# A fused attention and recurrent layer: where the sums of projection weight blocks are made

## The chip, the cores and the metric

The kernel runs on one core of a Trainium2 chip. The metric is the device time of one execution in microseconds (us). The engines are TensorE (PE for its matmuls, PEld for its weight loads), VectorE (DVE), ScalarE (ACT), GpSimd (POOL) and SyncE (SP); SP issues most DMAs, POOL the rest.

## The reference

One decoder layer on a sequence of 512 tokens with a width of 1024, in float32:

```python
h = rmsnorm(x, norm_mix_g)
q, k, v, xr, gr, g_attn, g_rnn = split(h @ w_in)              # 7 x 1024 columns
attn_out = diff_attention(q, k, v, ...)                       # 8 heads
rnn_out  = rg_lru_branch(xr, gr, conv_w, ..., w_a, w_x, ...)  # conv, two block-diagonal gates, scan, gelu
y_attn = attn_out @ w_proj_attn                               # 1024 x 1024
y_rnn  = rnn_out @ w_proj_rnn
merged = sigmoid(g_attn) * y_attn + sigmoid(g_rnn) * y_rnn
x = x + merged @ w_out
x = x + relu(rmsnorm(x) @ w_up)**2 @ w_down                   # 1024 x 4096 and back
```

## The kernel before, in words

Every matrix operand is split into a high and a low part (`hi` is a cast to a shorter format, `lo = x - hi`), and a product is three matmuls: hi by hi, hi by lo, lo by hi (`mm3`). Weights arrive in units of 128 x 1024 floats, 512 KB. A unit goes through three steps: SP loads it into one of two buffers `wraw`, ACT casts it to `whi`, DVE subtracts to get `wlo`. There are four buffers for pairs of `whi` and `wlo`, and a pair is free again when the unit's matmuls are done.

The kernel has these stages in order: a head (loads, norm), the attention with the projections of q, k, v and the two merge gates (45 to 283 us of the profiled execution), the stretch behind the attention, here called the recurrent stage (function `recurrent`, 291.45 us to about 476 us), the product with `w_out` and the norm (to about 520 us), and the MLP (to the end).

The recurrent stage lays several streams of PE work beside each other: 16 column units of `w_in` for xr and gr (`x` and `g` in the string `seq`), the attention's projection (`y`), the matmuls of the recurrence's gates (`t`), the projection of the recurrent branch (`a`, `b`, `c`) and the first units of `w_out` (`o`). PE's order is written out by hand in `seq`. The order of DVE, ACT and SP comes from a planner (`Plan`): each task has an engine, a duration, the tasks it follows, and places that it takes (2 of "raw" for the `wraw` buffers, 4 of "unit" for the pairs, 8 of "bank" for the accumulators `acc`). It computes when each task is due for PE, lays the tasks out by that, tries random changes, and emits the instructions in the order of the best layout. All engines then run their instructions in that fixed order and wait on semaphores. `HOPS` and `MARGIN` are the planner's cost of going from engine to engine and its reserve ahead of PE; `dve` and `act` are its durations.

The attention's projection (`project`) multiplies by blocks: the weight of one half of the output columns is four blocks b0, b1, b2, b3 (`w_pa[n, 0..3]`, each one unit), and instead of eight block products it takes seven, M1 to M7. M1, M2 and M3 use the plain blocks b0, b2 and b3. The other four use sums of blocks: M5 is b0+b1, M6 is b0+b1+b3, M4 is b0+b1+b3+b2, M7 is b1+b3. The matching sums of the activations (`early`, `third`, `pair_forms`) are made on DVE.

In the kernel before, POOL makes the sums of the weights while the attention runs. `add_up` loads a block from `w_pa` into an SBUF tile `sum`, adds the next block by an accumulating DMA into the same tile, and stores the tile to DRAM tensors `pa0M5`, `pa0M6` and so on (lists `pa_sums`). One generator per half takes turns (`in_turn`, `pas`), one step at a time, at fixed points of `qkv_pair` and `attention`. That makes 12 loads and 8 stores of 512 KB. In the recurrent stage each half then loads seven units: three plain ones and four finished sums.

A similar chain on POOL, `weight_sums`, makes 12 sums for the MLP's first weight with 18 loads and 12 stores into `up2M`, `up4M`, `up6M`. It starts behind the first convolution step of chunk 0 (`first` in `chunk`, line 1215). Its SBUF tile `sum` lies in a pool that is closed behind the recurrent stage.

The recurrence's gate weights come in four pairs of loads of 128 KB, one pair per chunk of the recurrent width (`graw`, line 1194). They land in a buffer of their own, `graw`, and are cast to `gw0` on ACT and subtracted to `gw1` on DVE.

Of the kernel before, what the change touches and what calls it, by code (L numbers as in the profile page):

```python
# [13 lines left out]
F32 = mybir.dt.float32  # L14
# [7 lines left out]
P = 128  # L22
# [17 lines left out]
def tile_block(ctx: ExitStack, tc: tile.TileContext, x, w_in, w_rga, w_rgx, w_pa, w_pr, w_o,  # L40
# [7 lines left out]
    sm = ctx.enter_context(tc.tile_pool(name="sm", bufs=4))  # L48
# [167 lines left out]
    def in_turn(*gs):  # L216
        gs = list(gs)
        while gs:
            g = gs.pop(0)
            if next(g, gs) is not gs:  # L220
                gs.append(g)
                yield

# [56 lines left out]
    ORDER_Y = ("M1", "M2", "M5", "M6", "M7", "M3", "M4")  # L280
    PLAIN = {"M1": 0, "M2": 2, "M3": 3}
# [9 lines left out]
    pa_sums = [{p: dp.tile([P, 1024], F32, name=f"pa{n}{p}") for p in ("M5", "M7", "M6", "M4")} for n in range(2)]  # L291
# [13 lines left out]

    def add_up(w, into):
        t = unit("sum", F32).rearrange("p c s -> p (c s)")
        for blocks in CHAINS:
            for b, p in blocks:
                if p:  # L310
                    G.dma_start(t, w[b], accum_op=ALU.add)
                    yield
                    G.dma_start(into[p], t)
                else:
                    G.dma_start(t, w[b])
                yield
# [224 lines left out]
    def qkv_pair(j, qk, v):  # L541
# [50 lines left out]
        for o, qi, gsc in ((OK_, 1, kg), (OQ, 0, qg), (OV, None, None)):  # L592
            t = -1
            for more in proj(o, banks[o]):
# [25 lines left out]
                if j == 0 and t % 2 == 1:  # L620
                    next(pas)
# [3 lines left out]
    def attention(fills, qks, vs, pads):  # L625
# [176 lines left out]
        for step in range(max(acts) + 1):  # L802
# [10 lines left out]
            for n, f in enumerate(order):  # L813
# [140 lines left out]
    HOPS = lambda x, t: 0.06 + (MARGIN if t.engine == "PE" else 0.0) if x.engine != t.engine else x.us - x.land  # L954
    MARGIN = 0.7
    dve = lambda columns: 0.08 + 0.00107 * columns
    act = lambda columns: 0.1 + 0.00085 * columns

    def recurrent(rp):
# [10 lines left out]
        class Unit:  # L970


            def __init__(self, src, shift, have=None, raw=None):
                self.raw, self.pair = raw, have
# [6 lines left out]
                if have or raw:  # L981
                    load.begun = -20.0
# [7 lines left out]
            def high(self):  # L990
                self.pair = weight_pair(self.shift)
                A.copy(self.pair[0], self.raw)
# [1082 lines left out]
```

## Time and profile before

| what | value |
|---|---|
| times of three runs | 836.78, 839.27 and 2138.16 us, median 839.27 |
| time of the profiled execution | 834.94 us, its span 833.2 us |
| granted TensorE clock | 1.00 |
| PE busy, share of the span | 824.5 us, 99% |
| DVE busy | 678.0 us, 81% |
| ACT busy | 502.4 us, 60% |
| POOL busy | 113.2 us, 14% |
| recurrent stage, 291.45 to 475.70 us | PE 181.81 of 184.25 us, DVE 155.05, ACT 119.26 |
| POOL's loads from `w_pa` in the attention | 12, first issued at 53.3 us, last at 143.2 us |
| POOL's loads from `w_up` in the recurrent stage | 18, first issued at 303.2 us, last at 464.8 us |

The table is read by stage. A busy time of PE below the stage's length is time in which PE waited for something; the trace's view of waits names what ended each such wait. Busy times of DVE and ACT say how much those engines have to do beside PE in the same stretch, not whether they are on the path.

### The profile page before, as it was taken

Reading aid. Unit: us, or ns where it says so; the run is one execution under the profiler, and the core shown is the slowest. Engines: PE = TensorE matmul, PEld = TensorE weight load, DVE = VectorE, ACT = ScalarE, POOL = GpSimd, SP = SyncE. Lnnn points to the kernel's source line nnn. Section 1 sums busy time; section 2 is a strip of 40 time slices with the busy share of each in tenths; the row PEclk is TensorE's granted clock in tenths of the full one; section 3 lists DMA queues with packets and bytes.
Section 4 is the critical chain, followed back from the end, with each engine's and each line's share of the span. In section 5 each row is a group of like instructions: output and inputs, shape, how many; then the busy total and the mean of one; then the engine's idle time right before and its main releaser. Section 6 shows DMA issues by size and latency. Waiting matters only on the chain.

```text
span 833.2 us, 14735 instructions
## 1 busy us (share of the span) xinstructions
PE 824.5 (99%) x5788; PEld 763.1 (92%) x5788; DVE 678.0 (81%) x1092; ACT 502.4 (60%) x791; POOL 113.2 (14%) x146
## 2 busy tenths in 40 slices
PE   9999999999999999999999999999999999999998
PEld 7899999999888888888887888799999999999998
DVE  6776788988966387799788867899889969976996
ACT  7445476666655254678766345784488348645852
POOL 0053333313000201101110000000000000000000
PEclk9999999999999999999999999999999999999999
DMA  6359885733432457687767662355655576556564
GB/s 205 125 180 283 258 229 126 190 96 89 115 89 69 110 150 216 210 231 207 215 204 194 183 227 76 102 152 152 209 151 148 157 253 173 140 168 199 153 165 113
DMA packets 49075, 139.77 MB, mean 168 GB/s; under 512 B 9111, under 2 KB 13919, under 8 KB 49006
## 3 DMA queue, kind: packets, MB, share of 16 engines
q1 hardware_dynamic: 36720, 97.64, 36.5%
q0 software_dynamic: 12272, 41.18, 21.6%
q8 instruction: 45, 0.74, 0.3%
q14 instruction: 24, 0.20, 0.1%
q10 hardware_dynamic: 14, 0.01, 0.0%
HBM read 111.50 MB, written 15.26 MB: 152 GB/s over the span
## 4 chain that ended last, share of the span: by engine, by line
PE 83%; DVE 9%; ACT 3%; DMA 3%; issue 2%; ACTq 0%; DVEq 0%
PE acc L69 51%; PE acc L152 8%; PE acc L151 8%; PE acc L153 8%; DVE wlo L69 3%; PE at L639 2%; PE at L151 1%; DMA wraw<-in_w_in_dram 1%; PE at L152 1%; PE at L153 1%; ACT whi L69 1%; PE at L673 1%; DMA wraw<-in_w_pr_dram 1%; PE at L568 1%; DVE pe L69 1%
## 5 line engine op out<-in xcount | busy, mean ns | idle before, releaser
L69 ACT CAST whi<-raw 128x1024 fp32r<-128x1024 f32 x109 | 112.4, 1050 | 94.1 <-DVE raw L69 36.6
L69 PE MATMUL acc<-h,whi 128*128 128x256 f32 (+1 forms) x851 | 154.0, 285 | 0.0
L69 PE MATMUL acc<-us,whi 128*128 128x256 f32 x900 | 153.2, 276 | 0.0
L69 DVE TENSOR_TENSOR wlo<-raw,whi 128x1024 fp32r<-128x1024 f32 x109 | 131.1, 1220 | 18.9 <-ACT whi L69 18.9
L69 DVE TENSOR_TENSOR wlo<-wraw,whi 128x1024 fp32r<-128x1024 f32 (+2 forms) x92 | 105.1, 1152 | 40.4 <-ACT whi L69 39.7
L69 PEld LDWEIGHTS acc<-us,whi 128*128 128x128 f32 x900 | 135.5, 188 | 0.0
L69 PEld LDWEIGHTS acc<-h,whi 128*128 128x128 f32 x851 | 130.7, 188 | 3.0 <-DVE h L69 0.5
L69 PE MATMUL acc<-us,wlo 128*128 128x256 f32 x448 | 123.6, 276 | 0.0
L69 PE MATMUL acc<-h,wlo 128*128 128x256 f32 (+1 forms) x424 | 120.8, 285 | 0.0
L69 ACT CAST whi<-wraw 128x1024 fp32r<-128x1024 f32 (+2 forms) x92 | 90.0, 988 | 44.6 <-PE acc L69 21.2
L151 PE MATMUL acc<-whi,hT 128*128 128x256 f32 x384 | 109.2, 284 | 0.0
L152 PE MATMUL acc<-wlo,hT 128*128 128x256 f32 x384 | 107.4, 280 | 0.2 <-DVE wlo L69 0.2
L69 PEld LDWEIGHTS acc<-us,wlo 128*128 128x128 f32 x448 | 84.1, 188 | 0.0
L69 PEld LDWEIGHTS acc<-h,wlo 128*128 128x128 f32 x424 | 79.6, 188 | 1.5 <-DVE wlo L69 0.3
L153 PE MATMUL acc<-whi,hT 128*128 128x256 f32 x288 | 80.5, 280 | 0.0
L152 PEld LDWEIGHTS acc<-wlo,hT 128*128 128x128 f32 x384 | 72.6, 189 | 0.5 <-DVE wlo L69 0.4
L151 PEld LDWEIGHTS acc<-whi,hT 128*128 128x128 f32 x384 | 72.3, 188 | 0.5 <-issue 0.2
L69 PE MATMUL acc<-hT,whi 128*128 128x512 f32 x224 | 71.7, 390 | 0.7 <-DVE xc L69 0.7
L69 POOL DMA_DIRECT2D raw<-raw x24 | 20.7, 862 | 321.3 <-DVE raw L69 127.6
L69 POOL TENSOR_TENSOR rs<-ms,mhalf 128x8 f32<-128x8 f32 (+1 forms) x25 | 39.2, 1568 | 170.4 <-DVE ms L69 170.3
L153 PEld LDWEIGHTS acc<-whi,hT 128*128 128x128 f32 x288 | 54.2, 188 | 0.0
L69 ACT ACTIVATE pe<-pe,nm 128x128 f32<-128x128 f32 (+3 forms) x64 | 35.6, 559 | 25.7 <-DVE nm L69 25.7
(240 smaller groups left out, 1816.9 us busy)
## 6 DMA issues: line engine op xcount, KB each, us to landing
wraw<-in_w_in_dram SPq DMA_DIRECT2D x54, 512.0 KB, 4.5
raw<-in_w_dn_dram SPq DMA_DIRECT2D x32, 512.0 KB, 4.2
raw<-in_w_up_dram SPq DMA_DIRECT2D x29, 512.0 KB, 4.2
raw<-raw POOLq DMA_DIRECT2D x24, 512.0 KB, 4.5
sum<-in_w_up_dram POOLq DMA_DIRECT2D x18, 512.0 KB, 5.7
sum<-in_w_pa_dram POOLq DMA_DIRECT2D x12, 512.0 KB, 7.0
wraw<-in_w_pr_dram SPq DMA_DIRECT2D x8, 512.0 KB, 4.8
wraw<-in_w_o_dram SPq DMA_DIRECT2D x8, 512.0 KB, 4.2
```

What stands on the lines that cost most here:

```text
L69: ins = f(*a, **k)
L151: T.matmul(o, l[0], r[0], start=first, stop=False)
L152: T.matmul(o, l[0], r[1], start=False, stop=False)
L153: T.matmul(o, l[1], r[0], start=False, stop=last)
L568: T.transpose(out=ps[:, t * P:(t + 1) * P], in_=qn[t // 2][:, c0:c0 + P], identity=ident)
L639: T.matmul(lg[c][:, :N], qT[:, c, i * P:(i + 1) * P], qk[h % 2, z][:, c, :N], start=z == 1, stop=z == 2)
L673: T.transpose(out=tp[:, b * P:(b + 1) * P], in_=st[s][:, b * P:(b + 1) * P], identity=ident)
```

## The change

The 12 loads and 8 stores of `add_up` are gone from POOL, with `in_turn`, `add_up`, `pa_sums` and the calls of `next(pas)`. In the recurrent stage a new generator `projection_units` makes the sums. Per half of the columns it loads five blocks: b0 into a tile of its own (`grown[n]`, named `wx` in the program), b2 as an ordinary unit for M2, b1 and b3 into `wraw` buffers, and b2 once more into a `wraw` buffer. DVE then adds in place: b0+b1 gives M5, adding b3 gives M6, b1+b3 (in b1's buffer) gives M7, adding b2 gives M4. These are four additions of 128 x 1024 a half (`added`). b1 and b3 keep their `wraw` buffers until the units made from them are split. The order of the products stays M1, M2, M5, M6, M7, M3, M4 in each half.

The gate weights lose their own buffer: `graw` takes one of the two `wraw` buffers, with the planner's hold "raw" for it. `weight_sums` starts behind the first convolution step of chunk 1 instead of chunk 0. The planner's numbers change (`HOPS`, `MARGIN`, `dve`, `act`, a load's landing 4.4 to 5.6 us, extra times `more=` for several operations, 400 tries instead of 800), the string `seq` is changed near its end, the casts into `R` wait for other tasks, the small-tile pool `sm` is closed ahead of the recurrent stage, and `wb.fetch()` is called right behind it.

```diff
-    def add_up(w, into):
-        t = unit("sum", F32).rearrange("p c s -> p (c s)")
-        for blocks in CHAINS:
-            for b, p in blocks:
-                if p:
-                    G.dma_start(t, w[b], accum_op=ALU.add)
-                    yield
-                    G.dma_start(into[p], t)
-                else:
-                    G.dma_start(t, w[b])
-                yield
...
-                    next(pas, None)
...
-    HOPS = lambda x, t: 0.06 + (MARGIN if t.engine == "PE" else 0.0) if x.engine != t.engine else x.us - x.land
-    MARGIN = 0.7
-    dve = lambda columns: 0.08 + 0.00107 * columns
-    act = lambda columns: 0.1 + 0.00085 * columns
+    HOPS = lambda x, t: 0.06 + (MARGIN if t.engine == "PE" else 0.0) if x.engine != t.engine else x.us - x.land + (0.116 if t.engine == "DVE" else 0.09)
+    MARGIN = 0.5
+    dve = lambda columns: 0.06 + 0.00106 * columns
+    act = lambda columns: 0.09 + 0.00084 * columns
...
-                load = plan.task("SP", 0.1, self.load, (), 4.4, takes=self.held[:1])
-                self.cast = plan.task("ACT", act(1024), self.high, (load,), takes=self.held[1:])
+                if of is None:
+                    after = [plan.task("SP", 0.1, self.load, (), 5.6, takes=self.held[:1])]
+                self.cast = plan.task("ACT", act(1024), self.high, after, takes=self.held[1:])
...
+        grown = [rp.tile([P, 4, 256], F32, tag=t, name="wx", bufs=b) for t, b in (("R", 8), ("wx", 1))]
...
+        class Raw:
+            def __init__(self, src, into=None, after=()):
+                self.t, self.src, self.held = into, src, plan.hold("raw")
+                self.came = plan.task("SP", 0.1, self.load, after, 5.6, takes=() if into is not None else (self.held,))
+            def load(self):
+                if self.t is None:
+                    self.t = wp.tile([P, 4, 256], F32, tag="wraw", name="wraw", bufs=2)
+                nc.sync.dma_start(self.t, self.src.rearrange("p (k c) -> p k c", k=4))
+        def added(x, y, after):
+            t = plan.task("DVE", dve(1024), lambda: V.tensor_tensor(out=x.t, in0=x.t, in1=y.t, op=ALU.add), [y.came, x.came, *after])
+            y.held.users.append(t)
+            return t
+        def projection_units(n):
+            X = Raw(w_pa[n, 0], grown[n], ())
+            whole = lambda r, *after: Unit(None, 0, of=lambda: r.t, after=after)
+            u = {"M1": whole(X, X.came)}
+            yield "M1", u["M1"]
+            yield "M2", Unit(w_pa[n, 2], 0)
+            b1 = Raw(w_pa[n, 1])
+            x = added(X, b1, [u["M1"].low, u["M1"].cast])
+            u = whole(X, x)
+            yield "M5", u
+            b3 = Raw(w_pa[n, 3])
+            y = added(X, b3, [u.low, u.cast])
+            m6 = whole(X, y)
+            yield "M6", m6
+            z = added(b1, b3, [x])
+            u = whole(b1, z)
+            b1.held.users += [u.cast, u.low]
+            yield "M7", u
+            u = whole(b3, b3.came)
+            b3.held.users += [u.cast, u.low]
+            yield "M3", u
+            b2 = Raw(w_pa[n, 2])
+            y = added(X, b2, [m6.low, m6.cast])
+            u = whole(X, y)
+            sums_done.append(u)
+            yield "M4", u
...
-                gw["raw"] = rp.tile([P, 2, 2, P], F32, tag="graw", name="graw")
+                gw["raw"] = wp.tile([P, 4, 256], F32, tag="wraw", name="wraw", bufs=2)[:, :2].rearrange("p z (n f) -> p z n f", n=2)
...
-            load = plan.task("SP", 0.3, graw, [prior[0].get("glow")], 2.5)
+            graws = plan.hold("raw")
+            load = plan.task("SP", 0.3, graw, [prior[0].get("glow")], 2.5, takes=[graws])
             gh = A_(ghigh, [load, *prior[0].get("gates", ())])
             gl = V_(glow, [gh])
+            graws.users += [gh, gl]
...
-                    if j == c == 0:
+                    if j == 1 and c == 0:
                         weight_sums(d[0]["xc"])
...
-                r1 = A_(kh, [i_, None if t < 2 else ys[11] if t < 6 else ys[11]])
+                r1 = A_(kh, [i_, None if t == 0 else sums_done[0].low if t == 1 else ys[11]])
...
-        seq = 'xx gg xx yy g y g tttt y x y x yy g tttt y g y x y x y g tttt y g yy aaa tttt a b c bc bc bc ooo'
+        seq = 'xx gg xx yy g y g tttt y x y x yy g tttt y g y x y x y g tttt y g yy aa tttt aa b c bc bc bc ooo'
...
+    es_sm.close()
...
     wb.ahead, wb.raws = 3, 2
+    wb.fetch()
     es_act.close()
```

The order of the instructions on three engines shows what this does. A number behind a name tells buffers of one kind apart. First POOL, at the head of the attention, in the kernel before: `rs` are the inverse norms for q and k, `qkT` moves rows of the transposed q and k, and the rest are the steps of `add_up`.

```order
L69 TENSOR_TENSOR rs_589<-ms,mhalf 128x8
L69 DMA sum<-in_w_pa_dram 128x1024
L69 TENSOR_TENSOR rs_649<-ms,mhalf 128x8
L69 DMA sum<-in_w_pa_dram 128x1024
L69 TENSOR_TENSOR rs_731<-ms,mhalf 128x8
L69 DMA sum<-in_w_pa_dram 128x1024
L69 DMA qkT<-qkT 64x512 x2
```

The same place on POOL in the changed kernel:

```order
L70 TENSOR_TENSOR rs_581<-ms,mhalf 128x8
L70 TENSOR_TENSOR rs_639<-ms,mhalf 128x8
L70 TENSOR_TENSOR rs_719<-ms,mhalf 128x8
L70 DMA qkT<-qkT 64x512 x2
L70 TENSOR_TENSOR rs_793<-ms,mhalf 128x8
L70 DMA qkT<-qkT 64x512 x2
```

The loads into `sum` have gone from between the inverse norms and the moves of `qkT`; nothing else moved there.

Second SP, in the recurrent stage around the first sums, in the kernel before. `in_w_in_dram` are column units for `x` and `g`, `graw` the gate weights in their own buffer, `pa0M5` and `pa0M6` the finished sums.

```order
L988 DMA wraw_3933<-in_w_pa_dram 128x1024
L988 DMA wraw_3975<-in_w_in_dram 128x1024
L988 DMA wraw_4011<-pa0M5_86 128x1024
L1197 DMA graw_4027<-in_w_rga_dram 128x2x128
L1197 DMA graw_4027<-in_w_rgx_dram 128x2x128
L988 DMA wraw_4034<-pa0M6_88 128x1024
L988 DMA wraw_4104<-in_w_in_dram 128x1024
```

The changed kernel at the same place. `wraw_3967` is b1 of the first half, `wraw_4035` the gate weights of chunk 0, `wraw_4081` b3.

```order
L964 DMA wraw_3879<-in_w_pa_dram 128x1024
L964 DMA wraw_3922<-in_w_in_dram 128x1024
L1090 DMA wraw_3967<-in_w_pa_dram 128x1024
L1223 DMA wraw_4035<-in_w_rga_dram 128x2x128
L1223 DMA wraw_4035<-in_w_rgx_dram 128x2x128
L1090 DMA wraw_4081<-in_w_pa_dram 128x1024
L964 DMA wraw_4138<-in_w_in_dram 128x1024
```

Plain blocks stand where the finished sums stood, and the gate weights of chunk 0, which SP issued ahead of the stage before, now stand between b1 and b3 and take a `wraw` buffer.

Third DVE, in the kernel before, from the split of the unit for M5 (`wlo_4063`) on. `wlo` are the low parts of units, `af` and `ag` forms of the activations' sums, `xl` the low part of the convolved input.

```order
L69 TENSOR_TENSOR wlo_4063<-wraw_4011,whi_4062 128x1024
L69 TENSOR_TENSOR af_3721<-tt1_4032,af_3721 128x2x256
L69 TENSOR_TENSOR xl_4069<-xc_3886,xh_4068 128x512
L69 TENSOR_TENSOR yq_4102<-acc_3906,yq_4102 128x512
L69 TENSOR_TENSOR aT_3265<-ae_3977,aT_3265 128x256
L69 SCALAR_TENSOR_TENSOR gate_452<-gate_452,yq_4102 128x2x256
L69 TENSOR_TENSOR ae_4113<-tt0_4009 128x256
L69 TENSOR_TENSOR xl_4073<-xc_3850,xh_4072 128x512
L69 TENSOR_TENSOR ae_4113<-tt0_4019,tt1_4032 128x256
L69 TENSOR_TENSOR wlo_4120<-wraw_4104,whi_4119 128x1024
```

The changed kernel on DVE, likewise from the split of the unit for M5 (`wlo_4042`) on. `wx_3689` is the tile that grows from b0 to the sum of all four blocks, `gw1` the low part of the gate weights.

```order
L70 TENSOR_TENSOR wlo_4042<-wx_3689,whi_4041 128x1024
L70 TENSOR_TENSOR ag_3696<-ae_4044,ag_3696 128x256
L70 TENSOR_TENSOR gw1_4049<-wraw_4035,gw0_4048 128x512
L70 TENSOR_TENSOR ae_4044<-tt0_3926,tt1_3965 128x256
L70 SCALAR_TENSOR_TENSOR q_3963<-q_3963,acc_3794 128x512
L70 TENSOR_TENSOR aT_3619<-ae_4044,aT_3619 128x256
L70 SCALAR_TENSOR_TENSOR q_3960<-q_3960,acc_3795 128x512 x2
L70 TENSOR_TENSOR wx_3689<-wx_3689,wraw_4081 128x1024
L70 TENSOR_TENSOR wlo_4095<-wraw_4081,whi_4094 128x1024
L70 TENSOR_TENSOR wraw_3967<-wraw_3967,wraw_4081 128x1024
L70 TENSOR_TENSOR wlo_4130<-wx_3689,whi_4129 128x1024
```

Behind the split of M5 there now stand the split of the gate weights, the additions of b3 into `wx` and into b1's buffer, and then the splits of M3 (`wlo_4095`) and M6 (`wlo_4130`).

More of the change, by code (lines that the diff above doesn't have):

```diff
@@ L981, in __init__ @@
                 if have or raw:
-                    load.begun = -20.0
+                    after[0].begun = -20.0
                 if have:
@@ L991, in high @@
                 self.pair = weight_pair(self.shift)
+                if self.of:
+                    self.raw = self.of()
                 A.copy(self.pair[0], self.raw)
@@ L1026, in unit_of @@
             return Unit(wb_reqs[n][0][0], wb_reqs[n][1], wb.units[n] if n < n_have else None, wb.raw[n] if n < n_raw else None)
-        V_ = lambda go, after, columns=512: plan.task("DVE", dve(columns), go, after)
-        A_ = lambda go, after, columns=512: plan.task("ACT", act(columns), go, after)
+        V_ = lambda go, after, columns=512, more=0.0: plan.task("DVE", dve(columns) + more, go, after)
+        A_ = lambda go, after, columns=512, more=0.0: plan.task("ACT", act(columns) + more, go, after)
         scaled = [V_(last_scaled[0], ()), None, None]
@@ L1230, in xlow @@
                     V.tensor_tensor(out=d[c]["x2"][1], in0=d[c]["xc"], in1=d[c]["x2"][0].bitcast(F32), op=ALU.subtract)
-                x = A_(first, [xs[1], was.get("xc")])
+                x = A_(first, [xs[1], was.get("xc")], more=0.07)
                 for n in range(3):
-                    x = V_(lambda n=n, tap=tap: tap(n), [x])
+                    x = V_(lambda n=n, tap=tap: tap(n), [x], more=0.05)
                 xbank.users.append(x)
@@ L1288, in roots @@
                     A.activation(d[c]["ae"], d[c]["ae"], AF.Sqrt, scale=-0.25)
-            root = plan.task("ACT", 2 * act(512) + 2.6, roots, [tail[0][0], tail[1][0]])
+            root = plan.task("ACT", 2 * act(512) + 2.75, roots, [tail[0][0], tail[1][0]])
             for c in both:
@@ L1375, in recurrent @@
             h = plan.hold("raw"), plan.hold("unit")
-            load = plan.task("SP", 0.1, lambda: wb.fetch_one(), (), 4.4, takes=h[:1])
+            load = plan.task("SP", 0.1, lambda: wb.fetch_one(), (), 5.6, takes=h[:1])
             cast = plan.task("ACT", act(1024), lambda: wb.cast(lates), [load], takes=h[1:])
@@ L1392, in recurrent @@
         slots[0] = 4
-        plan.run(dict(zip(("PE", "DVE", "ACT", "SP"), (*(0.0, 1.0, 1.0), 0.0))), 800)
+        plan.run(dict(zip(("PE", "DVE", "ACT", "SP"), (*(0.0, 1.0, 1.0), 0.0))), 400)
     def gate(dst, js):
@@ L1405, in tile_block @@
     spg = softplus()
-    pas = in_turn(*(add_up(w_pa[n], pa_sums[n]) for n in range(2)))
     qks, vs = [{} for _ in range(4)], [[] for _ in range(4)]
```

37 lines of the change are left out of this document (13 added, 24 removed).

## The prediction

> **What bounds the kernel now.** I read the page's busy times first, then busy time by stage, then what PE waited for. The page, parts one and two:
>
> ```profile
> PE 824.5 (99%) x5788; PEld 763.1 (92%) x5788; DVE 678.0 (81%) x1092; ACT 502.4 (60%) x791; POOL 113.2 (14%) x146
> PEclk9999999999999999999999999999999999999999
> ```
>
> PE is busy for 824.5 of 833.2 us at full granted clock, so PE's own work is the bound. All time in which PE is idle is 8.7 us, about 1% of the span. The busy time by stage (window, its length, then PE, PEld, DVE, ACT, POOL, clock, DMA share, GB/s) says where these 8.7 us lie:
>
> ```profile
> 0.00:45.00 45.00, 43.65 (x210) 37.00 (x211) 32.97 (x52) 26.27 (x42) 3.34 (x13) 1.00 0.48 160
> 45.00:283.00 238.00, 236.99 (x1768) 221.49 (x1766) 181.75 (x451) 143.15 (x302) 68.07 (x78) 1.00 0.56 156
> 53.00:158.30 105.30, 104.84 (x877) 101.95 (x876) 81.66 (x205) 60.63 (x129) 41.51 (x45) 1.00 0.80 222
> 291.45:442.67 151.22, 148.78 (x814) 129.09 (x812) 127.52 (x178) 102.47 (x142) 17.14 (x26) 1.00 0.71 204
> 442.67:475.70 33.03, 33.03 (x146) 27.33 (x147) 27.53 (x37) 16.80 (x22) 3.37 (x5) 1.00 0.65 180
> 480.00:520.00 40.00, 40.00 (x178) 33.14 (x177) 26.65 (x41) 20.50 (x29) 0.00 (x0) 1.00 0.45 158
> 520.00:833.20 313.20, 309.34 (x2625) 304.72 (x2623) 274.91 (x329) 190.90 (x252) 20.70 (x24) 1.00 0.57 162
> ```
>
> The attention leaves 1.0 us of idle PE, of which 0.5 us in the stretch in which POOL makes the sums (53.0 to 158.3). The recurrent stage leaves 151.22 - 148.78 = 2.4 us, all ahead of 442.67. The head (1.4) and the MLP with its end (3.9) are not touched by the change. The view of waits names the idle times:
>
> ```profile
> PE acc L69 <- DVE zero L69: 1.2, 1, 1.2
> PE acc L69 <- DVE q L69: 1.1, 1, 1.1
> PE acc L69 <- DVE xc L69: 0.7, 1, 0.7
> PE acc L69 <- ACT tt L69: 0.4, 1, 0.4
> PE at L152 <- DVE pt L69: 0.3, 1, 0.3
> ```
>
> The second to fourth are the recurrent stage's. PE waited there three times for DVE or ACT to free an accumulator or to deliver the gates' input, never for a weight unit. None of these waits is for a sum or for POOL. In the attention the one above 0.3 us is for DVE's `pt`.
>
> How fast PE runs there is read from the timeline (start, duration):
>
> ```profile
> 291.68 0.39 PE L69 MATMUL acc<-hT,whi 128*128 128x512 f32 x1
> 291.91 0.39 PE L69 MATMUL acc<-hT,wlo 128*128 128x512 f32 x1
> ...
> 324.08 0.28 PE L69 MATMUL acc<-aT,whi 128*128 128x256 f32 x1
> 324.19 0.28 PE L69 MATMUL acc<-aT,wlo 128*128 128x256 f32 x1
> 325.21 0.70 PE L69 MATMUL acc<-hT,whi 128*128 128x512 f32 x2 [0.73 <-DVE xc L69]
> ```
>
> From start to start a 512-column matmul takes 0.23 us (0.227 over the whole stage) and a 256-column one 0.11 (0.114). A column unit (24 matmuls) is 5.45 us, a projection product 2.74, a gate group (three matmuls) 0.68. A wait also costs the overlap: 324.19 + 0.11 = 324.30 was due, 325.21 came, 0.91 for a wait of 0.73. With about 0.17 of that per wait, the stage loses some 3 us to its waits.
>
> **PE's work.** The change gives PE the same units, products and gate groups in another order. Nothing of PE's 824.5 us goes. The most that any new layout can give is the waits of the attention's stretch and of this stage, 0.5 + 3 = 3.5 us, 0.4%.
>
> **What goes from the attention.** The tile view of `sum` (duration in ns min/median/max, first and last start):
>
> ```profile
> L69 POOL DMA_DIRECT2D sum<-in_w_up_dram x18: 527/867/911, 303.2 to 464.8; - x18
> L69 POOL DMA_DIRECT2D sum<-in_w_pa_dram x12: 540/902/972, 53.3 to 143.2; - x12
> L69 POOL DMA_DIRECT2D pa0M<-sum x4: 567/584/625, 71.0 to 152.2; - x4
> L69 POOL DMA_DIRECT2D up6M<-sum x4: 552/552/552, 431.8 to 473.0; - x4
> L69 POOL COPY sum<-xc x1: 183/183/183, 302.7 to 302.7; 128x1 f32<-128x1 f32 x1
> ```
>
> Gone are 12 issues of 0.90 and 8 of 0.58, 15.5 us of POOL, and 20 transfers of 512 KB in a stretch where the DMA engines are busy at 0.80. POOL has 41.51 of 105.3 us to do there and PE is idle for 0.46, so the gain has the ends 0 and 0.5 us. I take 0.2, since the one wait that is named there is for DVE.
>
> **What comes to DVE.** Prices and landings come from the tile views of `wraw` (291 to 443) and `graw`:
>
> ```profile
> L69 ACT CAST whi<-wraw x34: 1032/1048/1058, 292.1 to 438.9; 128x1024 fp32r<-128x1024 f32 x34
> L69 DVE TENSOR_TENSOR wlo<-wraw,whi x34: 1198/1221/1228, 293.2 to 440.2; 128x1024 fp32r<-128x1024 f32 x34
> DMA to landing us min/median/max: 3.5/4.4/7.4
> ...
> L1197 SPq DMA_DIRECT2D graw<-in_w_rgx_dram x4: 484/610/737, 276.1 to 383.6; - x4
> L69 ACT CAST gw<-graw x4: 618/619/631, 293.1 to 411.0; 128x512 fp32r<-128x512 f32 x4
> L69 DVE TENSOR_TENSOR gw<-graw,gw x4: 682/683/684, 320.8 to 412.3; 128x512 fp32r<-128x512 f32 x4
> DMA to landing us min/median/max: 5.4/5.4/5.5
> ```
>
> Eight additions of 128x1024, priced by the nearest row, the `wlo` with the same operands' shape: 8 x 1.22 = 9.8 us at most. DVE has 127.52 + 27.53 = 155.05 busy of 184.25 us, so about 165 of 184 after. It stays below PE, and the 29 us in which it sat idle cover the additions on the mean. Without that cover, at the places where DVE is last, each addition would cost its 1.2 us. Additions and splits alike are spread by the planner, so what counts is each unit's own chain.
>
> **The new chain through the two `wraw` buffers.** b1 keeps one from its load to the split of M7. Gate weights and b3 must follow each other through the other. I laid the instructions of all engines in the changed order by these durations (0 is the stage's first matmul); these sums are estimates. The tight places:
>
> M6 of the first half. `wlo_4004` ends at 32.5: 24.5 us of DVE instructions from the split of the third column unit on, which starts at about 8. Then the gate weights: landing 5.4, cast 0.6, split 0.6 with hops, so the buffer is free at 39.2. b3 lands 4.4 later (43.7), its addition ends at 44.9, `wlo_4095`, b1+b3 and `wlo_4130` follow, at 48.3. PE needs M6 after 7 column units, 3 products and 4 gate groups, 38.2 + 8.2 + 2.7 = 49.1. Spare: 0.8 us.
>
> The gates of chunk 2. The weights `wraw_4745` are issued at 108.4, when a buffer comes free; 5.4 + 0.6 + 0.6 gives 115.0. PE is there after 14 column units, 12 products and 8 gate groups: 114.6. A stall of 0 to 0.5. In the kernel before this load had its own buffer, and its cast ran long ahead.
>
> Then `wlo_4827` is ready 0.4 us ahead of PE, the low half of `R_5095` 0.9 late, `wlo_5189` 0.4 late, `wlo_5322` 0.2 late and `mT[4]` 0.7 late. All others are ahead by 1.4 us or more. Together the stalls are 2.2 to 2.7 us. They take the place of those before (3 us at `xc`, `tt` and `q`), whose gates now stand elsewhere in PE's order. One more or one less stall of 1 us is the uncertainty, so the stage's ends are +1 and -1.8. I take -0.5.
>
> **The later start of `weight_sums`.** Before, the chain runs from 303.2 to its last store's landing at 473.0 + 4.8:
>
> ```profile
> sum<-in_w_up_dram POOLq DMA_DIRECT2D x18, 512.0 KB, 5.7
> up6M<-sum POOLq DMA_DIRECT2D x4, 512.0 KB, 4.8
> ...
> 530.54 1.23 DVE L69 TENSOR_TENSOR wlo<-raw,whi 128x1024 fp32r<-128x1024 f32 x1 [0.40 <-ACT whi L69]
> ```
>
> That is 174.6 us for 18 loads and 12 stores one behind the other. The first convolution of chunk 1 comes at 51 us into the stage, so the chain runs from 342.5 to about 517. Its first reader in time is the instruction at 530.54, a split into memory that the tile `sum` leaves free; behind it on DVE stand the MLP's forms and splits, and PE waits for those. 13 us of spare: cost 0. The Trainium skill, "DMA: Bandwidth & Descriptors", section "Anatomy of one DMA — SWDGE (gpsimd) path", puts a DMA of this path at about 2.0 us and its bytes at 436 GB/s, by which 512 KB would be an estimated 3.2 us and the chain's 30 transfers 96 us, with 90 us of spare. The trace disagrees with its 5.7 and 4.8 us in a stage where the other loads run too, so the spare goes by the rows.
>
> The other changes on SP and POOL (fourteen projection loads become ten, `w_out` loads ahead of the load of `x`) move loads that PE does not wait for, since PE is full from 442.67 to 475.70 and from 480 to 520. Cost 0.
>
> **Sum.** 834.94 for the profiled execution - 0.2 (attention) - 0.5 (stage) = 834.2. The two close runs of the three, 836.78 and 839.27, lie 1.8 and 4.3 above the profiled one; I add the smaller: 836.0. A measurement of this kernel can tell about 2%, 16.7 us, from no change, and this is far below.
>
> **Rivals.**
>
> All waits go (B). The planner's new numbers lie nearer to the rows (a load lands in 5.6 instead of 4.4 by its account), for which speaks that they are safer; against it speaks that the gate weights are still planned at 2.5 against 5.4. Gain 3.5: 831.4 for the profile, 833 for the median.
>
> The two buffers decide (C). If loads land at the row's 7.4 instead of 4.4, each tight place is 3 us later less its spare: M6 2.2, chunk 2 3.0, `wlo_4827` 2.6, the place with 1.4 spare 1.6, and one later 3.0. Together 12 us: 848, slower but below 2%. It starts to cost once a landing is 0.8 us over the median. For it: two buffers carry 36 loads in both kernels, and now two are held for long. Against: the DMA share falls where POOL's chain starts 40 us later.
>
> The sums come late (D). It decides from 13 us of delay on: each of the 30 transfers 0.45 us slower. Then the split at 530.54 waits, and each further us costs up to one. Slower by 2% takes a chain of 205 us and more, 1.0 us per transfer. In a POOL of 0.53 to 0.91 us per issue beside a DVE at 84% no row shows such a delay. If each issue were held by one DVE instruction of 1.22 us, it would be 37 us, an end at 554, 24 late: about 855 to 859 us. The trace does not bear such a hold out: the issues stay below one `wlo`. The Trainium skill, "SBUF — State Buffer", section "Who interferes with whom", says that a DVE instruction with two inputs in SBUF contends with a GpSimd instruction that reads SBUF, which would speak against the change if a DMA's issue were one; no row here shows what an issue reads.
>
> The change does nothing at all (E): the attention's DMAs were hidden and the stage's waits only change names. That is 836.5, and lies within the forecast.
>
> **How the numbers follow.** Forecast with E: 0.62, 836. B: 0.15, 833. C: 0.16, 840 to 848. D: 0.04, above 853. Small other stalls of the new layout: 0.03. The range takes in B's 831.4 less 1 for the spread of the runs (830.5) and of C the lower part (844). Faster by over 2% is out of reach with PE's work unchanged: 0.01. Slower by over 2% is D and the upper end of C: 0.06. Same: 0.93.
>
> **What would show it.** In the changed kernel: PE's busy time again 824 to 825 us; POOL without `sum<-in_w_pa`, and the idle PE in 53 to 158 below 0.5; three or more short waits of PE between the stage's first matmul and 185 us later, with 2 to 4 us in total; `wraw<-in_w_rga` landing in 5 to 6 us; DVE 160 to 167 us busy in the stage; the last `up6M` store issued near 512. Waits of PE for `gw` or for the `wlo` behind an addition, with loads landing at 6 us and more, would show C; a DVE `wlo` at about 530 released by POOL's or a DMA's end would show D. PE busy by less or more than 1 us against before would make the sum wrong at its root.

## The result and the profile after

The changed kernel takes 845.77 us (median of five, 845.23 to 847.11), the kernel before 837.57 us. The ratio is 1.010, with a 95% interval of 1.0081 to 1.0118; one execution of the kernel before that took 2138.16 us is no part of it. It is about 8 us slower, inside the 2% that was forecast as most likely, but above the range, which ended at 844. The direction was wrong too: 836 was forecast.

The profiled execution took 845.23 us, with a span of 843.5. Its page, parts one and two:

```profile
PE 837.0 (99%) x5788; PEld 774.2 (92%) x5788; DVE 685.8 (81%) x1100; ACT 501.5 (59%) x791; POOL 99.3 (12%) x126
PEclk9999999999999999999999999999999999999999
```

PE executes the same 5788 instructions at the same full granted clock, but it is busy for 837.0 us instead of 824.5. That is 12.5 us more of PE's own time, which is more than the whole loss. The waits of PE, where a stall would show:

```profile
PE acc L70 <- DVE zero L70: 1.2, 1, 1.2
PE acc L70 <- ACT h L70: 0.5, 1, 0.5
PE at L649 <- DVE pe L70: 0.2, 1, 0.2
PE acc L70 <- DVE h L70: 0.2, 1, 0.2
PE at L152 <- ACT hu L70: 0.2, 1, 0.2
PE acc L153 <- DVE wlo L70: 0.2, 1, 0.2
```

The recurrent stage's three waits (1.1, 0.7, 0.4) are gone, and none of the tight places of the prediction shows one. The lost time is in no wait. To find it, I cut both spans at the same matmuls. All numbers are starts of a matmul, taken from the trace, and their differences in us:

| stretch | before | changed | difference |
|---|---|---|---|
| start to the attention's first projection | 40.76 | 41.01 | +0.25 |
| attention, to its last product with `v` | 235.56 | 234.98 | -0.58 |
| recurrent stage, to the first product with `w_out` | 199.84 | 198.44 | -1.40 |
| product with `w_out` | 43.52 | 43.56 | +0.04 |
| MLP, up to the first matmul that streams `us` | 41.78 | 43.90 | +2.12 |
| MLP, from there to the last matmul | 267.66 | 277.75 | +10.09 |
| last matmul to the end | 4.07 | 3.84 | -0.23 |

The change gains 1.7 us up to the MLP, in the places where it was meant to act. It then loses 12.2 us in the MLP, of which it changes no line. The busy times of the MLP's last stretch, the first row of the kernel before and the second of the changed one (window, length, then PE, PEld, DVE, ACT, POOL with their instructions, clock, DMA share, GB/s):

```profile
561.45:829.10 267.65, 267.65 (x2360) 267.65 (x2359) 235.75 (x280) 158.75 (x202) 18.09 (x21) 1.00 0.59 168
```

```profile
561.88:839.62 277.74, 277.74 (x2360) 277.74 (x2359) 236.57 (x279) 158.92 (x201) 18.10 (x21) 1.00 0.57 162
```

PE is never idle in either stretch, its instructions are the same 2360, and the clock is 1.00 in both. DVE, ACT and POOL are busy for nearly the same time, and the DMA share differs by 0.02. Yet a matmul takes 267.65 / 2360 = 113.4 ns before and 277.74 / 2360 = 117.7 ns after. The timeline of the changed kernel shows it, where a step from one row's start to the next is one matmul or two:

```profile
639.75 0.28 PE L70 MATMUL acc<-h,wlo 128*128 128x256 f32 x1
639.87 0.40 PE L70 MATMUL acc<-h,whi 128*128 128x256 f32 x2
640.11 0.28 PE L70 MATMUL acc<-h,wlo 128*128 128x256 f32 x1
640.23 0.40 PE L70 MATMUL acc<-h,whi 128*128 128x256 f32 x2
```

The first and third rows are 0.36 us apart, three matmuls at 120 ns. The kernel before at the same time, with matmuls of the same shape:

```profile
639.88 0.28 PE L69 MATMUL acc<-us,wlo 128*128 128x256 f32 x1
639.99 0.39 PE L69 MATMUL acc<-us,whi 128*128 128x256 f32 x2
640.22 0.28 PE L69 MATMUL acc<-us,wlo 128*128 128x256 f32 x1
```

Here three matmuls take 0.34 us, 113 ns each.

What is different for these matmuls is where their operands lie: the streamed one, whose columns pass through PE, and the stationary one, which a weight load puts into PE first. The change closes the pool `sm` (1344 bytes a partition) ahead of the recurrent stage to make room for the tile `wx`. The pools `rp` and `fin` that follow then start 1344 bytes lower. The compiled programs have these start addresses, in bytes within a partition:

```
pool and tile                              before    changed
rp   R (recurrent branch, streamed)         86912      85568
fin  h2 (MLP input, streamed)               86912      85568
fin  us (MLP inner, streamed)              171136     169792
fin  whi (MLP weight pair, stationary)     220544     219200
hp   us (MLP inner, streamed)               52544      52544
wp   whi (four weight pairs, stationary)    17728      17728
```

1344 is 5 x 256 + 64. Where one operand of a matmul lies in a pool that moved and the other in one that did not, their distance (stationary minus streamed address) has changed by 64 modulo 256. In the kernel before, all 2520 matmuls of 256 columns of the MLP have a distance of 64. In the changed kernel 912 still have it, 1476 have 128 and 132 have 0.

### The profile page after: what moved, and what is told of

The parts are those of the page before. It is cut to its first block, busy times and chain, and to the rows that moved or that the text cites. A ratio compares the mean times of both kernels' runs of the same rounds, so it can differ in the third digit from the quotient of the medians.

```text
span 843.5 us, 14702 instructions
## 1 busy us (share of the span) xinstructions
PE 837.0 (99%) x5788; PEld 774.2 (92%) x5788; DVE 685.8 (81%) x1100; ACT 501.5 (59%) x791; POOL 99.3 (12%) x126
## 4 chain that ended last, share of the span: by engine, by line
PE 86%; DVE 8%; ACT 3%; issue 2%; DMA 1%; SPq 0%; ACTq 0%; DVEq 0%
PE acc L70 58%; PE acc L152 6%; PE acc L153 6%; PE acc L154 6%; PE at L615 2%; DVE wlo L70 2%; PE at L152 1%; PE at L154 1%; PE at L153 1%; DMA wraw<-in_w_o_dram 1%; PE at L649 1%; DVE gate L70 1%; ACT whi L70 1%; PE at L546 1%; DVE pe L70 1%
## 5 line engine op out<-in xcount | busy, mean ns | idle before, releaser
L70 PE MATMUL acc<-h,whi 128*128 128x256 f32 (+1 forms) x851 | 159.6, 290 | 0.7 <-ACT h L70 0.5
L70 PE MATMUL acc<-us,whi 128*128 128x256 f32 x900 | 158.8, 280 | 0.0
L70 PEld LDWEIGHTS acc<-us,whi 128*128 128x128 f32 x900 | 137.9, 188 | 0.0
L70 PEld LDWEIGHTS acc<-h,whi 128*128 128x128 f32 x851 | 132.5, 188 | 4.3 <-ACT h L70 0.9
L70 PE MATMUL acc<-us,wlo 128*128 128x256 f32 x448 | 125.7, 280 | 0.0
L70 PE MATMUL acc<-h,wlo 128*128 128x256 f32 (+1 forms) x424 | 122.6, 289 | 0.0
L70 DVE TENSOR_TENSOR wlo<-wraw,whi 128x1024 fp32r<-128x1024 f32 (+2 forms) x84 | 95.2, 1145 | 27.8 <-ACT whi L70 27.3
L70 ACT CAST whi<-wraw 128x1024 fp32r<-128x1024 f32 (+2 forms) x84 | 81.7, 981 | 24.3 <-PE acc L70 11.9
```

What stands on the lines that cost most here:

```text
L70: ins = f(*a, **k)
```

## The experiments

Theory A: PE's time per matmul depends on the distance between the addresses of its streamed and its stationary operand, and the closing of `sm` has moved them against each other. Theory B: the order of the work, the transfers or the later weight sums slow PE down. Theory C: any other place would do.

**A gap of 64 bytes.** An unused tile ahead of the two pools in the changed kernel restores every distance modulo 256.

```diff
+    ctx.enter_context(tc.tile_pool(name="gap", bufs=1)).tile([P, 16], F32, name="gap")
     with tc.tile_pool(name="rp", bufs=1, reuse_waits="tile") as rp:
```

> The changed kernel with an unused tile of 64 bytes a partition ahead of the pools rp and fin, nothing else. Theory A (the pools' start addresses have moved by 1344 bytes, an odd number of 64-byte steps, and PE takes 118 instead of 113 ns for a 256-column matmul where streamed and stationary operand start at the same address modulo 128): the MLP's matmuls go back to 113.4 ns, PE busy falls from 837 to about 824, the time to 833-836. Theory B (the order of work, the transfers or the later weight sums make PE slow): no change, 844-847.

Measured: 835.17 us beside 839.97 for the kernel before on the same chip, ratio 0.9946 (0.9929 to 0.9962). The MLP's last stretch:

```profile
559.01:827.95 268.94, 268.70 (x2361) 268.30 (x2359) 235.71 (x280) 158.75 (x202) 18.05 (x21) 1.00 0.59 167
```

The matmuls are back at 268.70 / 2361 = 113.8 ns, and this stretch is 8.8 us shorter than in the changed kernel. The changed kernel's 845.77 us comes from another session; against the 846.59 us of the next experiment, from the same session, the 64 unused bytes bring 11 us. The changed kernel then beats the one before by half a per cent. The order of work, the transfers and the later sums are all still there, so theory B is out.

**A gap of 128 bytes.** The same place with twice the size.

```diff
+    ctx.enter_context(tc.tile_pool(name="gap", bufs=1)).tile([P, 32], F32, name="gap")
     with tc.tile_pool(name="rp", bufs=1, reuse_waits="tile") as rp:
```

> The changed kernel with an unused tile of 128 bytes ahead of rp and fin. Theory A: addresses move but stay as they are modulo 128, so the time stays 844-847 and the 256-column matmuls of the MLP at 117-118 ns. Theory C (any other start address than the changed kernel's would do, or a coarser raster counts): faster, 833-840. Theory B: 844-847.

Measured: 846.59 us, ratio 1.0075 (1.006 to 1.009). The last stretch takes 278.89 us, 118 ns a matmul. The addresses moved (1475 of the MLP's matmuls now have a distance of 0) and the loss stayed, so theory C is out.

**The gap in the kernel before.** The same 64 bytes there, and nothing of the change.

```diff
+    ctx.enter_context(tc.tile_pool(name="gap", bufs=1)).tile([P, 16], F32, name="gap")
     with tc.tile_pool(name="rp", bufs=1, reuse_waits="tile") as rp:
```

> The kernel before with an unused tile of 64 bytes ahead of rp and fin. Theory A: the MLP's 256-column matmuls go from 113.4 to about 118 ns, and the kernel before becomes 10-13 us slower, 847-851, with nothing of the change in it. Theory B: no change, 836-839.

Measured: 854.04 us, ratio 1.0164 (1.0149 to 1.0179). The last stretch:

```profile
567.75:846.64 278.89, 278.89 (x2360) 278.89 (x2359) 236.39 (x279) 159.09 (x201) 18.10 (x21) 1.00 0.58 161
```

The kernel before gets the MLP's slow matmuls, 118.2 ns, from a tile that nobody uses. It loses 14 us in the medians, above the 10 to 13 expected. The profiled execution shows where: 11.2 us in this stretch, 1.7 ahead of it in the MLP and 3.8 in the recurrent stage, where a wait of PE for `xc` grew from 0.7 to 2.0 us and, as the last section shows, PE ran at half its clock for 3.4 us behind it.

**The gap ahead of the MLP's pool alone.** The tile stands in front of `fin`, and `rp` stays where the change puts it.

```diff
+    ctx.enter_context(tc.tile_pool(name="gap", bufs=1)).tile([P, 16], F32, name="gap")
     fin = ctx.enter_context(tc.tile_pool(name="fin", bufs=1, reuse_waits="tile"))
```

> The changed kernel with the 64 bytes ahead of fin alone (MLP), rp (recurrent stage) left as the change puts it. Theory A: nearly all of the loss is the MLP's, so 833-837, up to 2 us above the kernel with the gap ahead of both. Theory B: 844-847.

Measured: 835.44 us, ratio 0.9947 (0.9933 to 0.9962). So nearly all of the loss was the MLP's. About 1.3 us were the recurrent stage's: the 192 matmuls of 512 columns that stream `R` start 235 ns apart here, as in the changed kernel, and 227 ns apart with the gap ahead of both pools. The timed runs do not tell this from nothing (835.44 against 835.17).

**Moving the stationary side instead.** No gap; the MLP's weight pairs in `wp` start 64 bytes lower.

```diff
-            units[o] = weight_pair((0 if own else 64) if o[0] != "pl" else 192 if own else 0, fin if own else None)
+            units[o] = weight_pair(0 if o[0] != "pl" else 192 if own else 0, fin if own else None)
```

> The changed kernel without any gap; only the stationary side moves: the MLP's weight pairs in the pool wp start 64 bytes lower (shift 0 instead of 64), so that 672 instead of 1609 of the MLP's 2518 matmuls of 256 columns have both operands at the same address modulo 128. Theory A1 (the relation of both addresses counts): 4 to 5 of the MLP's 12 us of loss remain, 837-842, and matmuls streaming h at about 113-115 ns. Theory A2 (the streamed operand's own address counts): 844-847, matmuls at 117-118 ns.

Measured: 840.81 us, ratio 1.0018 (0.9999 to 1.0038). The last stretch takes 272.19 us, 4.5 us above the kernel before, where 4 to 5 were expected. In the trace the 1848 matmuls whose distance is now 64 have a median of 113 ns and the 672 others, at a distance of 0, 119 ns, side by side in one execution with nothing streamed from a new place. So it is not the streamed operand's own address that counts. Nor is it the stationary operand's own: the gaps left the pairs in `wp` where they were and changed their matmuls' time. It is the distance of the two.

**Steps of 32 bytes.** Gaps of 32 and of 96 bytes in the changed kernel (8 elements as shown, and 24).

```diff
+    ctx.enter_context(tc.tile_pool(name="gap", bufs=1)).tile([P, 8], F32, name="gap")
     with tc.tile_pool(name="rp", bufs=1, reuse_waits="tile") as rp:
```

> The changed kernel with a gap of 32 bytes ahead of rp and fin: in most of the MLP the stationary operand lies 96 bytes (modulo 256) above the streamed one, where the changed kernel has 128 and the kernel before 64. If the time of a matmul falls off on both sides of 64: 115-117 ns, 838-843. If whole steps of 64 bytes count: 113-114 ns and 833-836, or 118-120 ns and 844-848.

> The changed kernel with a gap of 96 bytes: the stationary operand lies 32 bytes above the streamed one. If the time falls off on both sides of 64: 115-117 ns, 838-843. If whole steps of 64 bytes count, this or the kernel with a gap of 32 bytes is at 113-114 ns and 833-836, and the other at 118-120 ns.

Measured: 848.23 us (ratio 1.0108, 1.0073 to 1.0142) and 846.71 us (1.0099, 1.0067 to 1.013), with the last stretch at 277.43 and 278.01 us. Neither expectation held. The time does not fall off gently around 64, and it is no matter of whole steps of 64 bytes, or one of the two would have been fast. A distance of 64 is the one good value among the eight seen. From the records of eight kernels (both, and the experiments so far that moved addresses, without the fourth), between 300 and 840 us, median start-to-start time in ns by the distance (stationary minus streamed address, modulo 256; the addresses are those of the compiled programs, whose matmuls stand in the order of the trace's):

| distance | 0 | 32 | 64 | 96 | 128 | 160 | 192 | 224 |
|---|---|---|---|---|---|---|---|---|
| 256 columns | 120 | 117 | 114 | 119 | 119 | 119 | 118 | 117 |
| how many | 4008 | 1606 | 11403 | 1591 | 2027 | 144 | 1824 | 144 |
| 512 columns | 227 | 235 | 235 | - | - | - | 231 | 234 |
| how many | 5264 | 290 | 580 | 0 | 0 | 0 | 580 | 290 |

256-column matmuls were fastest at a distance of 64, 512-column ones at 0. Theory A first had a modulus of 128; 192 is as slow as the others, which speaks for 256. The entries of 256 columns at 160, 192 and 224 come from the attention's projection alone, though, and no run had a 64 there. In these 540 us the kernel before has 0 for all its matmuls of 512 columns, and 64 for all of 256 columns but the 336 of the attention's projection, which lie at 192.

A distance of 64 is no guarantee, though. With the gap of 128 bytes, 372 matmuls of the MLP at 64 stand in short groups between others of 118 to 120 ns, and their median was 118 ns too. And in the kernel without additions (below), where all 2520 lie at 64, PE changed its pace behind a wait of 0.8 us at 614.52 and changed back some 50 us later. Two stretches of that trace, the one behind the wait first:

```profile
614.60:666.00 51.40, 51.40 (x437) 51.40 (x438) 46.53 (x54) 37.02 (x50) 3.52 (x5) 1.00 0.53 154
668.00:730.00 62.00, 62.00 (x548) 62.00 (x547) 51.07 (x57) 41.69 (x55) 4.29 (x5) 1.00 0.61 171
```

That is 117.6 and 113.1 ns a matmul at one distance and one clock. So PE kept the longer time there for hundreds of matmuls; what starts and ends such a stretch is open.

**The start of the MLP's sums.** The changed kernel with the gap, and `weight_sums` back behind chunk 0.

```diff
-                    if j == 1 and c == 0:
+                    if j == c == 0:
                         weight_sums(d[0]["xc"])
```

> The changed kernel with the gap of 64 bytes and with the start of the MLP's weight sums put back behind chunk 0's convolution. If the later start costs nothing and saves nothing: ratio to the kernel before as with the gap alone, 0.994-0.996, recurrent stage 165-167 us from first aT product to first mT product. If the earlier chain makes the projection's loads land late in the two buffers: 1 to 4 us more, stage 167-170 us, ratio 0.996-1.0.

Measured: 833.29 us, ratio 0.9936 (0.9912 to 0.9961). This is not told apart from the gap alone, and the first expectation came. In one profiled execution each, the recurrent stage is 1.3 us longer than with the later start (198.41 against 197.14) and the MLP's first stretch 0.9 us shorter (41.75 against 42.64). The early start does not cost what the second expectation put on late loads (ratio 0.996 to 1.0). The three versions with the gap and the change's own plan beat both kernels of the case.

**The planner's numbers on the kernel before.** `HOPS`, `MARGIN`, `dve`, `act`, the landings of 5.6, the `more=` terms, 400 tries and the new `seq`, with sums, buffers and addresses as before. Its core:

```diff
-    MARGIN = 0.7
-    dve = lambda columns: 0.08 + 0.00107 * columns
-    act = lambda columns: 0.1 + 0.00085 * columns
+    MARGIN = 0.5
+    dve = lambda columns: 0.06 + 0.00106 * columns
+    act = lambda columns: 0.09 + 0.00084 * columns
...
-                load = plan.task("SP", 0.1, self.load, (), 4.4, takes=self.held[:1])
+                load = plan.task("SP", 0.1, self.load, (), 5.6, takes=self.held[:1])
```

> The kernel before with the change's planner numbers, PE order and number of tries, its own sums and buffers kept, and addresses as before. Theory P (the 2.7 us that the recurrent stage gains with the gap come from the planner's numbers): stage 165-167 us, ratio 0.995-0.998. Theory Q (they come from the units' new order and the sums that need no finished store): stage 168-169 us, ratio 0.999-1.001.

Measured: 843.28 us, ratio 1.0047 (1.0027 to 1.0067). Neither theory's ratio came. But the recurrent stage, measured like the table above from the attention's last product (the first product with `aT`, from which the expectation measures, comes later in this layout), takes 197.11 us, as short as with the whole change:

```profile
278.19:475.30 197.11, 196.81 (x1032) 168.66 (x1030) 155.16 (x218) 121.87 (x171) 23.67 (x34) 1.00 0.69 192
```

PE is idle for 0.3 us there, against 2.5 before. What this kernel gained it more than lost elsewhere. The attention, which this edit leaves alone, ended 1.9 us later in this execution, and the MLP's first stretch took 49.35 us instead of 41.78, with a wait of 3.7 us for ACT's `h` (until 528.53) and half the granted clock behind it:

```profile
528.60:533.00 4.40, 4.40 (x10) 3.19 (x11) 4.30 (x6) 3.35 (x5) 0.00 (x0) 0.50 0.20 31
```

Why ACT came late there, though not in the changed kernel, was not followed up.

**The old planner's numbers under the new sums.** The reverse: the changed kernel with the gap, planner's numbers, tries and `seq` of before.

```diff
-    MARGIN = 0.5
+    MARGIN = 0.7
...
-                self.came = plan.task("SP", 0.1, self.load, after, 5.6, takes=() if into is not None else (self.held,))
+                self.came = plan.task("SP", 0.1, self.load, after, 4.4, takes=() if into is not None else (self.held,))
...
-        V_ = lambda go, after, columns=512, more=0.0: plan.task("DVE", dve(columns) + more, go, after)
+        V_ = lambda go, after, columns=512, more=0.0: plan.task("DVE", dve(columns), go, after)
```

> The changed kernel with the gap of 64 bytes, and the planner's numbers, PE order near the end and number of tries of the kernel before; sums on DVE and shared buffers stay. Theory P (the recurrent stage's gain is the planner's): from the attention's last product to the first mT product 198.5-201 us instead of 197.1, ratio 0.996-1.0. Theory Q (it is the new sums and order of units): 197-198 us, ratio 0.994-0.996.

Measured: 846.23 us, ratio 1.0089 (1.0061 to 1.0117). The recurrent stage takes 215.34 us instead of 197.14. Its waits:

```profile
PE acc L70 <- ACT tt L70: 10.6, 4, 5.4
```

The granted clock was 0.50 for 17 us in and behind these waits, and PE is busy for 204.25 us in the stage instead of 196.44. The profiled execution was the slowest of the six; the medians, 846.23 against 835.17 from another session, differ by 11 us. The ratio lies outside both theories. It lies on the side of P: with the old numbers the planner did not find an order of the new work that keeps PE fed. Which of the numbers does it (the landing of 4.4, the costs, the tries, `seq`) was not separated, and the next experiment shows that a layout can miss by several us for smaller reasons.

**Without the additions.** The changed kernel with the gap, whose eight additions are planned as tasks of no length and not emitted.

```diff
-            t = plan.task("DVE", dve(1024), lambda: V.tensor_tensor(out=x.t, in0=x.t, in1=y.t, op=ALU.add), [y.came, x.came, *after])
+            t = plan.task("DVE", 0.0, lambda: None, [y.came, x.came, *after], land=0.0)
```

> The changed kernel with the gap of 64 bytes and without DVE's eight additions, so that the sums of the projection's weights are left out; loads, buffers and splits stay. If the additions lie in DVE's idle time: the same time as with them, 833-836, and DVE 9 to 10 us less busy. If they are last ahead of PE's products: up to 3 us less.

Measured: 843.58 us, ratio 1.0055 (1.0033 to 1.0078): slower with less work, and neither expectation. DVE is busy for 155.68 us in the recurrent stage instead of 164.50. But the planner, given other durations, found another layout, with waits of 2.5 us for `tt` and 3.8 us for `h`, and the MLP had the stretch of 50 us at 117.6 ns shown above. The run says nothing about the price of the additions. It says that a new layout by this planner varies by more than they cost.

**The attention without its transfers.** The kernel before without `add_up`; the four units of a half that were sums are plain blocks, so the sums of the projection's weights are left out.

```diff
-    pas = in_turn(*(add_up(w_pa[n], pa_sums[n]) for n in range(2)))
+    pas = iter(())
...
-                unit = Unit(w_pa[n, PLAIN[p]] if p in PLAIN else pa_sums[n][p], 0)
+                unit = Unit(w_pa[n, PLAIN.get(p, 1)], 0)
```

> The kernel before without the 20 POOL transfers of the attention; the four units of a half that were sums are loaded as plain blocks, so the sums of the projection's weights are left out. Theory: the transfers were hidden, the attention gets 0 to 0.6 us shorter, ratio 0.999-1.000. Rival: fewer transfers leave PE a higher granted clock or free DVE, ratio 0.995-0.997.

Measured: 837.09 us beside 839.86, ratio 0.9966 (0.9945 to 0.9986). The attention takes 234.84 us instead of 235.56, and in the stretch from 53 to 158.3 us PE is idle for 0.07 instead of 0.46:

```profile
53.00:158.30 105.30, 105.23 (x878) 102.68 (x877) 82.20 (x205) 60.92 (x130) 28.62 (x26) 1.00 0.45 129
```

The trace accounts for 0.7 us of the 2.8 by which the medians differ. The ratio is the rival's and not the theory's, but neither of the rival's causes shows: the mean granted clock over all timed runs is 0.9988 for both kernels, and DVE is busy for 82.20 us in the stretch, not less than the 81.66 before. The rest is open: the profiled execution has an `xc` wait of 2.2 us in the recurrent stage, and the timed runs of both kernels spread over 7 us.

## Why the prediction was wrong

The step that failed is **PE's work**: "The change gives PE the same units, products and gate groups in another order. Nothing of PE's 824.5 us goes." The matmuls are the same, as forecast, but the time of one is not: 117.7 instead of 113.4 ns in the MLP. I read the matmuls' start-to-start times as constants of the shape, though the trace of before already held two values for 256 columns. In the recurrent stage the matmuls that stream `aT` start 118 ns apart (distance 192), and those of the MLP 113 ns apart (distance 64). The rows that I quoted, rounded to 10 ns, hide this; the medians over the records show it. The prediction's own check ("PE busy by less or more than 1 us against before would make the sum wrong at its root") was the one that fired. The line responsible, `es_sm.close()`, was in the diff and in the description; I had priced it at nothing as a matter of room. The kernel held a hint as well: `weight_pair(shift)` puts a unit 0, 64 or 192 bytes into its tile, a choice that changes addresses and no value.

The other steps, point by point:

- **What goes from the attention**: -0.2 forecast, -0.58 measured, against an upper end of 0.5. Removing the transfers alone gives -0.7 in the trace, and 2.8 in the medians, which stay unexplained. The idle PE fell from 0.46 to 0.08 us.

```profile
53.00:158.30 105.30, 105.22 (x881) 102.70 (x880) 82.10 (x205) 61.09 (x130) 28.63 (x26) 1.00 0.44 128
```

- **The recurrent stage**: -0.5 forecast with ends of +1 and -1.8. It measured -1.4 as it is, and -2.7 with the addresses restored (197.14 against 199.84; 198.41 with the early sums), in one execution each. Its waits are gone, as rival B had it. The planner's new numbers alone give the same 2.7; the new sums under the old numbers take 18 us more in the profiled execution.
- **The new chain through the buffers**: laid almost as it came, with two sizes off. M6 was laid ready at 48.3 us into the stage and PE there at 49.1; they came at 47.5 and 49.4. I took 5.4 us for every landing of gate weights. In the changed kernel the known landings differ:

```profile
L1223 SPq DMA_DIRECT2D wraw<-in_w_rga_dram x4: 378/379/379, 323.6 to 423.1; - x4
L1223 SPq DMA_DIRECT2D wraw<-in_w_rgx_dram x4: 463/484/842, 324.1 to 423.5; - x4
...
DMA to landing us min/median/max: 2.2/2.4/4.8
```

  The 2.2 is chunk 0's (2.6 us from the first of its two issues), so M6 had more to spare, and the 2.4 is chunk 3's. The 4.8 is chunk 2's: 5.2 us from the first issue, nearly as priced, and ACT's cast waited for it:

```profile
399.55 0.38 SPq L1223 DMA_DIRECT2D wraw<-in_w_rga_dram  x1
404.86 0.62 ACT L70 CAST gw<-wraw 128x512 fp32r<-128x512 f32 x1 [4.98 <-DMA wraw<-in_w_rgx_dram]
405.51 0.69 DVE L70 TENSOR_TENSOR gw<-wraw,gw 128x512 fp32r<-128x512 f32 x1 [2.02 <-ACT gw L70]
407.09 0.40 PE L70 MATMUL acc<-xh,gw 128*128 128x512 f32 x1
```

  The split ended 115.1 us into the stage, where 115.0 was laid. The stall of 0 to 0.5 did not come because PE got there at 116.0 and not at 114.6: its products take 118 to 120 ns a matmul, where the prediction had 114, and 12 products of 24 matmuls make about 1.2 us of that. The step that failed hid this one. Rival C's landings of 7.4 us did not occur; between 323 and 424 us the longest that is known was 5.5.
- **What comes to DVE**: eight additions at 1.22, as priced. DVE's busy time in the stage rises by 6 us (155.05 to 161.25), not by the 9.8 of the eight, and PE waits for none of them.

```profile
L70 DVE TENSOR_TENSOR wx<-wx,wraw x6: 1215/1221/1226, 324.1 to 417.1; 128x1024 f32<-128x1024 f32 x6
L70 DVE TENSOR_TENSOR wraw<-wraw x2: 1217/1219/1221, 334.8 to 394.4; 128x1024 f32<-128x1024 f32 x2
291.10:475.35 184.25, 184.15 (x966) 157.66 (x965) 161.25 (x221) 117.59 (x164) 17.19 (x26) 1.00 0.60 172
```

- **The later start of `weight_sums`**: the last store was issued at 503.0, where 512 was forecast, ahead of the reader at 530. Rival D did not come. Cost 0 was nearly right: PE waits 0.5 us for `h` at the MLP's start, and in the kernel with the gap and the early start no such wait is listed. That the later start causes it is not shown.
- **Rivals**: rival C's time (840 to 848) came, by another mechanism than rival C's. None of the rivals had a place for PE's own pace.

Without the loss in the MLP the time would have lain inside the range: the ratios of the versions with the gap (0.9936 to 0.9947) put it at 832 to 833 us beside 837.57, rival B's 833 rather than the 836 of the sum.

## What to carry to other kernels

A change that opens, closes or resizes a buffer pool moves every tile behind it. Before calling matmul work unchanged, compare the start addresses of streamed and stationary tiles in both programs, and look for two start-to-start times of one shape in the trace. When PE's busy time grows at the same instruction count and the same granted clock, look at addresses before looking at waits. And when a planner's layout is part of the change, its numbers are part of the change too: here they alone brought the recurrent stage's whole gain in one profiled execution.

## What the runs showed of the hardware

A matmul of 256 columns in this 32-bit format had a median of 113 to 114 ns when the stationary operand lay 64 bytes above the streamed one modulo 256, and of 117 to 120 ns at the seven other distances seen in steps of 32. One of 512 columns took a median of 227 ns at distance 0, and 231 to 235 at the four others seen. At 64, matmuls among others at a worse distance, or behind a short wait, could also take 118 ns, for 50 us in one trace. Weight loads run beside the matmuls all through the MLP (PEld is busy for as long as PE), so the two reads of PE may disturb each other, depending on how they fall in time; that is argued, since no run separated them.

A wait of PE also has a price behind it. After waits of 1.1 to 1.5 us, in five kernels, the granted clock stayed at 1.00. Here is the stretch behind the 1.1 us wait of the kernel before:

```profile
442.70:446.00 3.30, 3.30 (x14) 2.71 (x15) 2.95 (x5) 2.15 (x4) 0.00 (x0) 1.00 0.79 286
```

After the wait of 2.0 us in the kernel before with the gap (it ended at 327.22, and the low clock began 1.2 us later), and after 2.2 us in the kernel without the transfers:

```profile
328.50:331.80 3.30, 3.30 (x9) 2.60 (x8) 3.30 (x7) 1.42 (x2) 0.32 (x1) 0.50 0.93 303
```

```profile
326.20:329.50 3.30, 3.29 (x8) 2.62 (x9) 3.30 (x5) 1.93 (x4) 0.56 (x1) 0.50 0.98 339
```

After 2.5 us in the kernel without additions, and after 5.4 us in the one with the old plan:

```profile
442.80:445.00 2.20, 2.20 (x5) 1.75 (x6) 1.56 (x3) 1.56 (x4) 0.87 (x1) 0.50 0.84 231
```

```profile
387.10:391.00 3.90, 3.90 (x18) 3.90 (x19) 3.04 (x5) 3.87 (x6) 0.00 (x0) 0.50 0.70 129
```

So after every wait of 2.0 us and more in these traces PE ran at half its clock, for 3.4 us after waits of 2.0 to 2.5 us, and for 6.8 us, which in part still lay in the wait, with waits of 3.7, 3.8 and 5.4. Half the clock for 3.4 us adds about 1.7 us to the wait, an estimate from these figures. Waits between 1.5 and 2.0 us did not occur. The Trainium skill, "TensorE: Matmul & The Clock Gate", section "HAM oscillation — how this bites in real kernels", warns of idle gaps of PE above about 3.4 us; here 2.0 to 2.5 us were enough, and the measurement decides. Rival C, whose stalls of 2.2 to 3.0 us are of this length, was priced too cheaply for the case that it had come.
